# Building the state-space tables of the first stage on one engine, and modulating the tokens on another

## The chip, the cores and the metric

One core of a Trainium2 chip runs the kernel; the other seven are idle. The metric is the device time of one execution in microseconds (us), and the number quoted is the median of three executions.

## What is computed

One layer of a diffusion backbone on 256 latent tokens and 256 context tokens of width 2048, all in float32. The tokens are modulated by a conditioning vector, projected once, mixed by three branches in parallel (long convolution, chunkwise mLSTM, and a bidirectional complex-diagonal state-space model, S5), merged by gates, projected, normalised, and put through a squared-ReLU MLP. Cut to what matters here:

```python
mod_l = split(silu_c @ w_mod[l] + b_mod[l], 6)            # shift, scale, ...
mod_c = split(silu_cc @ w_mod[l] + b_mod[l], 6)
def modulate(h, shift, scale): return h * (1 + scale) + shift
h_ctx, h_lat = modulate(ctx, mod_c[0], mod_c[1]), modulate(x, mod_l[0], mod_l[1])
hy, qk, v, o, gt, u, mg = split(h @ w_in, SPLIT_POINTS)    # for both streams
ab, bb = s5_discretise(a_re, a_im, log_dt, b_re, b_im)     # per direction, group, state
s_t = ab * s_(t-1) + bb u_t;   y_t = Re(c s_t)             # S5, both directions
```

The kernel does the S5 recurrence in chunks of 8 tokens. For that it needs tables built from the weights alone: the complex powers ab^0 to ab^8 of each state, times c (the table Q) and times bb (the table w).

## The kernel before, in words

The work on each engine stands in a fixed order, which a scheduler chose when the kernel was built; each engine takes its instructions strictly in that order. Matrix products of the large projections are done as three products of rounded parts: a weight chunk is loaded by SyncE into a buffer `wr`, ScalarE copies it to its high part `wh`, VectorE subtracts to get the low part `wl`, and TensorE multiplies (`mm`, all at L211). The high part of anything is made at L190 (`act`), the low part at L194 (`split`).

The first stage is the first quarter of a millisecond. It runs three strands side by side:

- **Modulation vectors.** `mod_block` (L395 on) loads `w_mod` in chunks of 512 KB, eight to a block, into ten buffers (four `wr`, three `wh`, three `wl`), multiplies them by the conditioning vectors at L406, copies the result on ScalarE, transposes it with small products, and adds the bias on VectorE (L415, `modc`).
- **Tokens and the K projection.** After each two blocks a group g of four 128-channel slices of both streams can be modulated. `h_group` (L426 on) does this by eight VectorE instructions of 128x256 (L435, `ty<-ty,modc`), then makes four high parts on ScalarE and four low parts on VectorE (tile `t`, two KB wide streams `hc` and `hl`). There are four groups. Three K-projection steps of `w_in` (`part`, L1449 on) follow each group; their partial sums are added on VectorE at L1460.
- **S5 tables.** `s5_params` (L440 on) discretises. `s5_tables` (L540 on) then goes over six channel tiles, two halves of each, and two directions d. `powers` (L525) makes a piece of Q or w by four multiplications with a broadcast operand (L536, L537) and one addition (L538). Direction 0 runs on VectorE, direction 1 on GpSimd. TensorE multiplies Q by a small masked matrix `bb` (L564) and transposes w (L214); ScalarE copies the transposes to `s5wa`; Q goes to memory from GpSimd's queue (L568, tensor QD), the transposes from ScalarE's queue (L583, tensor WA).

The tables are a side strand: `chunk_done` advances them by one step per weight chunk, times a rate (1.0). They are not needed until the S5 branch, hundreds of microseconds later. After the stage, from about 240 us, TensorE runs almost without a pause to the end.

Of the kernel before, what the change touches and what calls it, by code (L numbers as in the profile page):

```python
# [17 lines left out]
P = 128  # L18
# [97 lines left out]
class Kern:  # L116
# [322 lines left out]

    def s5_params(self):  # L440
# [10 lines left out]
        self.work = [self.t(self.br, [P, 1152], f"s5t{d}", 1) for d in range(2)]  # L451
        tmp = self.slices(self.work[0][:, :1104].rearrange("p (a n) -> p a n", n=48))
# [51 lines left out]
        w1, w2 = (self.work[1][:, 384 * i:384 * i + 384].rearrange("p (q c) -> p q c", c=16) for i in range(2))  # L504
# [20 lines left out]
    def powers(self, out, m, d, q, l0, n):  # L525


        e = self.nc.vector if d == 0 else self.nc.gpsimd
        k = q.stop - q.start
        pw = self.pq[:, :, q, :] if d == 0 else self.pq[:, :, q, ::-1]  # L530
        pw = pw[:, :, :, l0:l0 + n]
        t = self.work[d][:, :k * 2 * n * 16].rearrange("p (q s l c) -> p q s l c", q=k, s=2, c=16)
        for s in range(2):
            bcp = lambda i: pw[:, i].unsqueeze(3).to_broadcast([P, k, n, 16])
            bcm = lambda i: m[:, i, q, :].unsqueeze(2).to_broadcast([P, k, n, 16])
            e.tensor_mul(out[:, :, s], bcp(1 + s), bcm(0))  # L536
            e.tensor_mul(t[:, :, s], bcp(s), bcm(1))  # L537
        e.tensor_add(out, out, t)  # L538

    def s5_tables(self):  # L540
# [3 lines left out]
        v = nc.vector  # L544
        for ct in range(CT):
            pk = self.aux([P, 2, P])
            for half in range(2):
                for d in range(2):
                    q = slice(24 * d + 4 * ct + 2 * half, 24 * d + 4 * ct + 2 * half + 2)
                    Q1 = self.t(self.br, [P, 576], f"s5Q{d}", 1)  # L550
                    Q = Q1.rearrange("p (q s n) -> p q s n", q=2, s=2)
                    self.powers(Q.rearrange("p q s (l c) -> p q s l c", c=16), self.s5C, d, q, 0, 9)
                    bb = self.t(self.br, [P, 2, 2, 32], "s5bb", 2)
                    nc.gpsimd.memset(bb, 0.0)
                    for h in range(2):

                        for s in range(2):
                            self.act(bb[64 * h:64 * h + 64, s, :, 16 * h:16 * h + 16],
                                     self.s5B[64 * h:64 * h + 64, s, q, :], scale=1.0 - 2.0 * s)
                    l0 = 0 if d == 0 else 16  # L560
                    for s in range(2):
                        for i in range(2):
                            p = 2 * half + i
                            nc.tensor.matmul(pk[32 * p:32 * p + 32, d, :], bb[:, s, i, :], Q[:, i, s, l0:l0 + P],  # L564
                                             start=d == 0 and s == 0, stop=s == 1, skip_group_check=True,
                                             tile_position=(0, 32 * p))
                    o = 16 - l0
                    nc.gpsimd.dma_start(self.QD[ct, d, :, 2 * half:2 * half + 2], Q[:, :, :, o:o + P])  # L568
                    yield
                wt = []  # L570
                for d in range(2):
                    q = slice(24 * d + 4 * ct + 2 * half, 24 * d + 4 * ct + 2 * half + 2)
                    w = self.t(self.br, [P, 2, 2, P], "s5w", 4)
                    self.powers(w.rearrange("p q s (l c) -> p q s l c", c=16), self.s5B, d, q, d, LC)
                    wt.append(w)
                for i in range(2):
                    wa = self.t(self.br, [P, 4, P], "s5wa", 2)
                    pt = self.aux([P, 4, P])
                    for d in range(2):
                        for s in range(2):  # L580
                            self.tr(pt[:, 2 * d + s, :], wt[d][:, i, s])
                    self.act(wa, pt)
                    nc.scalar.dma_start(self.WA[ct, :, 2 * half + i], wa)  # L583
                yield
            kk = self.t(self.br, [P, 15, 16], "s5kk", 2)
# [6 lines left out]
            yield  # L592
# [65 lines left out]
    def s5_output(self):  # L658
# [8 lines left out]
        for ct in range(CT):  # L667
# [3 lines left out]
            Q = self.t(self.br, [P, 2, 4, 2, P], "s5wq", 2)  # L671
            nc.scalar.dma_start(Q.rearrange("p d q s n -> p d (q s n)"),
                                self.QD[ct].rearrange("d p q s n -> p d (q s n)"))
# [9 lines left out]
            for d in range(2):  # L683
                for s in range(2):
                    for p in range(4):
                        o = 64 * (p % 2)
                        self.nc.tensor.matmul(py[o:o + 64, p // 2, :], xb[:, p, d, s].rearrange("p g j -> p (g j)"),
                                              Q[:, d, p, s, :], start=p < 2 and d == 0 and s == 0, stop=False,
# [885 lines left out]
```

## Time and profile before

| | us |
|---|---|
| median of 3 executions (lowest, highest) | 2039.77 (2035.3, 2040.7) |
| the profiled execution, its own time | 2046.25 |
| its span, from first to last instruction | 2044.3 |
| TensorE busy in the span | 1885.0 |
| VectorE busy | 1342.6 |
| ScalarE busy | 797.7 |
| GpSimd busy | 473.4 |

Busy time is the time in which an engine has an instruction under way, and an instruction that is held up after its start counts as busy. So a long mean for a shape that is short elsewhere is itself a wait. The last column of a group row gives the idle time of the engine just before the group and what ended it. The profiled execution is 6.5 us above the median.

### The profile page before, as it was taken

The numbers are of one execution on the slowest core, as the hardware profiler recorded it, in microseconds if no ns is written. First come the engines' busy times: TensorE is split into PE (matmuls) and PEld (weight loads), VectorE is DVE, ScalarE is ACT, GpSimd is POOL, SyncE is SP. The second block draws the span as 40 slices with busy tenths as digits, with TensorE's granted clock in tenths as the row PEclk, the third lists the DMA queues.
The fourth block names the chain that finished last, engine by engine and source line by source line (L and its number), as shares of the span: only waits on it lengthen the run. The fifth ranks groups of instructions, "written<-read, shape, count | busy, mean of one in ns | idle before, by whom it ended". The sixth has DMA issues, their size and how long they took to land.

```text
span 2044.3 us, 34693 instructions
## 1 busy us (share of the span) xinstructions
PE 1885.0 (92%) x13945; PEld 1716.5 (84%) x13945; DVE 1342.6 (66%) x1842; ACT 797.7 (39%) x1079; POOL 473.4 (23%) x654
## 2 busy tenths in 40 slices
PE   4787899999999896999889998899999999999996
PEld 1555888898998896999769977899989899998986
DVE  8789876655876564455777767866655555555556
ACT  1233333324544332534333443544343334444332
POOL 4777311000015997000343400500000000000001
PEclk8898899999999898999999999999999999999998
DMA  8798667766698675777756876577765566666653
GB/s 311 262 299 285 195 203 221 228 199 184 206 318 272 211 242 172 262 251 243 270 183 217 278 249 218 174 248 229 244 208 190 189 185 181 184 185 230 190 187 115
DMA packets 255200, 455.92 MB, mean 223 GB/s; under 512 B 28789, under 2 KB 75541, under 8 KB 253504
## 3 DMA queue, kind: packets, MB, share of 16 engines
q1 hardware_dynamic: 221824, 382.43, 59.0%
q0 software_dynamic: 12384, 44.54, 6.2%
q10 hardware_dynamic: 20832, 26.75, 3.9%
q8 instruction: 109, 1.79, 0.4%
q14 instruction: 51, 0.42, 0.1%
HBM read 424.75 MB, written 32.05 MB: 223 GB/s over the span
## 4 chain that ended last, share of the span: by engine, by line
PE 64%; DVE 14%; DMA 8%; POOL 8%; issue 4%; ACT 1%; ACTq 0%; POOLq 0%; DVEq 0%; SPq 0%
PE mm L211 57%; DMA wr<-in_w_mod_dram 4%; PE aux L211 4%; DVE wl L194 4%; POOL sc L654 2%; POOL sc L653 2%; POOL t L655 2%; POOL sc L652 2%; DVE t L194 1%; DMA wr<-in_w_in_dram 1%; DVE ty L435 1%; ACT wh L190 1%; DVE mac L1181 1%; DVE s5t L537 1%; DMA s5wq<-WA 1%
## 5 line engine op out<-in xcount | busy, mean ns | idle before, releaser
L211 PE MATMUL mm<-t,wh 128*128 128x256 f32 x5888 | 1102.7, 288 | 24.8 <-ACT wh L190 12.6
L211 PEld LDWEIGHTS mm<-t,wh 128*128 128x128 f32 x5888 | 933.7, 194 | 46.6 <-ACT wh L190 13.9
L194 DVE TENSOR_TENSOR wl<-wr,wh 128x1024 fp32r<-128x1024 f32 (+1 forms) x517 | 657.0, 1277 | 381.6 <-ACT wh L190 380.7
L211 PE MATMUL mm<-t,wl 128*128 128x256 f32 x2944 | 850.1, 289 | 23.3 <-DVE wl L194 23.0
L190 ACT ACTIVATE wh<-wr 128x1024 fp32r<-128x1024 f32 (+1 forms) x517 | 546.4, 1058 | 807.9 <-PE mm L211 577.6
L211 PEld LDWEIGHTS mm<-t,wl 128*128 128x128 f32 x2944 | 571.4, 194 | 37.4 <-DVE wl L194 29.4
L1181 DVE SCALAR_TENSOR_TENSOR mac<-wr,vecs,mac 128x512 f32<-128x512 f32 x240 | 186.8, 778 | 152.7 <-DMA wr<-in_w_mod_dram 150.0
L211 PE MATMUL mm<-wh,t 128*128 128x512 f32 (+1 forms) x960 | 249.3, 349 | 1.7 <-ACT wh L190 1.7
L211 PEld LDWEIGHTS mm<-wh,t 128*128 128x128 f32 x960 | 169.7, 191 | 25.6 <-ACT wh L190 2.7
L211 PE MATMUL mm<-wl,t 128*128 128x512 f32 (+1 forms) x480 | 169.2, 352 | 5.2 <-DVE wl L194 5.2
L211 PE MATMUL mm<-wh,ff 128*128 128x512 f32 (+1 forms) x576 | 155.3, 358 | 0.0
L211 PEld LDWEIGHTS mm<-wh,ff 128*128 128x128 f32 x576 | 101.8, 188 | 17.6
L211 PEld LDWEIGHTS mm<-wl,t 128*128 128x128 f32 x480 | 91.6, 191 | 21.7 <-DVE wl L194 10.5
L211 PE MATMUL mm<-wl,ff 128*128 128x512 f32 (+1 forms) x288 | 103.0, 357 | 0.0
L1403 POOL DMA_DIRECT2D t<-in_ln_g_dram x1 | 0.5, 535 | 358.8 <-PE mm L211 358.8
L211 PE MATMUL mm<-ty,wh 128*128 128x256 f32 x384 | 74.1, 291 | 0.0
L211 PE MATMUL mm<-ty,wl 128*128 128x256 f32 x192 | 57.0, 297 | 6.7 <-DVE wl L194 6.7
L211 PEld LDWEIGHTS mm<-ty,wh 128*128 128x128 f32 x384 | 61.6, 195 | 0.9
L211 PEld LDWEIGHTS mm<-wl,ff 128*128 128x128 f32 x288 | 54.2, 188 | 8.8
L1192 POOL DMA_DIRECT2D mrow<-b x8 | 4.0, 502 | 227.8 <-DVE b L1190 227.8
L211 PE MATMUL aux<-t,t 128*128 128x384 f32 (+3 forms) x160 | 48.8, 422 | 8.0 <-DVE t L1147 3.5
L406 PE MATMUL px<-wr,b 128*32 128x512 f32 x128 | 40.3, 714 | 12.9 <-DVE s5t L335 10.7
(389 smaller groups left out, 1813.6 us busy)
## 6 DMA issues: line engine op xcount, KB each, us to landing
wr<-in_w_ff_dram SPq DMA_DIRECT2D x256, 512.0 KB, 3.9
wr<-in_w_in_dram SPq DMA_DIRECT2D x192, 512.0 KB, 4.7
wr<-in_w_mod_dram SPq DMA_DIRECT2D x160, 512.0 KB, 4.8
wr<-in_w_out_dram SPq DMA_DIRECT2D x32, 512.0 KB, 4.9
wh<-in_w_mod_dram SPq DMA_DIRECT2D x16, 512.0 KB, 6.2
wl<-in_w_mod_dram SPq DMA_DIRECT2D x16, 512.0 KB, 7.8
QD<-s5Q POOLq DMA_DIRECT2D x24, 256.0 KB, 4.9
WA<-s5wa ACTq DMA_DIRECT2D x24, 256.0 KB, 5.2
```

Of the source, the lines that this page charges most:

```text
L190: return self.nc.scalar.activation(out, in_, f, bias=bias, scale=scale)
L194: self.nc.vector.tensor_sub(lo, x, hi.bitcast(F32))
L211: self.nc.tensor.matmul(out, lhsT, rhs, start=start, stop=stop, skip_group_check=True)
L406: nc.tensor.matmul(ps[o:o + 32], self.st[:, k, :], raw[:, kk, :], start=k < 4, stop=k >= KT - 4, skip_group_check=True, tile_position=(0, o))
L435: self.nc.vector.tensor_scalar(h[:, j], h[:, j], self.modc[:, 16 + k, m:m + 1], self.modc[:, k, m:m + 1], op0=ALU.mult, op1=ALU.add)
L537: e.tensor_mul(t[:, :, s], bcp(s), bcm(1))
L652: v.tensor_mul(t1, self.a8[:, 0], S[:, :, :, :, n - 1])
L653: v.tensor_mul(t2, self.a8[:, 1], S[:, :, ::-1, :, n - 1])
L654: v.tensor_add(t1, t1, S[:, :, :, :, n])
L655: v.tensor_add(S[:, :, :, :, n], t1, t2)
L1181: v.scalar_tensor_tensor(acc, x, c, acc, op0=ALU.mult, op1=ALU.add)
L1192: nc.gpsimd.dma_start(self.mrow[which // 3:which // 3 + 1, o:o + 512], brow)
```

## The change

All powers run on VectorE, in pieces of a whole channel tile (four state groups instead of two), for both directions. That makes half as many pieces, each twice as wide: multiplications of 128x576 and 128x512, additions of 128x1152 and 128x1024. GpSimd keeps the memsets of `bb` and the transfers of Q, and gets the transfers of the transposes (WA), which ScalarE's queue issued. The tokens are modulated on ScalarE by an activation with a scale and a bias per partition. The side strand's rate goes from 1.0 to 0.8; it has fewer steps. Buffers: two of 1152 columns for Q (one per direction of 576 before), two of 1024 for w (four of 512), one `s5kk` (two). The layout of QD in memory changes, and its readers with it. In the code of the change the lines of `powers` are L537, L538 and L539, the product is L566, the transfers L570 (QD) and L589 (WA).

```diff
                 for j in range(2):
                     k, m = k0 + j, 1 - s
-                    self.nc.vector.tensor_scalar(h[:, j], h[:, j], self.modc[:, 16 + k, m:m + 1],
-                                                 self.modc[:, k, m:m + 1], op0=ALU.mult, op1=ALU.add)
+                    self.act(h[:, j], h[:, j], AF.Identity, bias=self.modc[:, k, m:m + 1],
+                             scale=self.modc[:, 16 + k, m:m + 1])
                 self.split(hh[:, k0:k0 + 2, :], hlo[:, k0:k0 + 2, :], h)
...
-    def powers(self, out, m, d, q, l0, n):
+    def powers(self, out, m, d, ct, l0, n):
-        e = self.nc.vector if d == 0 else self.nc.gpsimd
-        k = q.stop - q.start
+        v = self.nc.vector
+        q = slice(24 * d + 4 * ct, 24 * d + 4 * ct + 4)
         pw = self.pq[:, :, q, :] if d == 0 else self.pq[:, :, q, ::-1]
         pw = pw[:, :, :, l0:l0 + n]
-        t = self.work[d][:, :k * 2 * n * 16].rearrange("p (q s l c) -> p q s l c", q=k, s=2, c=16)
+        t = self.work[:, :128 * n].rearrange("p (s q l c) -> p s q l c", s=2, q=4, c=16)
+        bcp = lambda i: pw[:, i].unsqueeze(3).to_broadcast([P, 4, n, 16])
+        bcm = lambda i: m[:, i, q, :].unsqueeze(2).to_broadcast([P, 4, n, 16])
         for s in range(2):
-            bcp = lambda i: pw[:, i].unsqueeze(3).to_broadcast([P, k, n, 16])
-            bcm = lambda i: m[:, i, q, :].unsqueeze(2).to_broadcast([P, k, n, 16])
-            e.tensor_mul(out[:, :, s], bcp(1 + s), bcm(0))
-            e.tensor_mul(t[:, :, s], bcp(s), bcm(1))
-        e.tensor_add(out, out, t)
+            v.tensor_mul(out[:, s], bcp(1 + s), bcm(0))
+            v.tensor_mul(t[:, s], bcp(s), bcm(1))
+        v.tensor_add(out, out, t)
...
         for ct in range(CT):
             pk = self.aux([P, 2, P])
-            for half in range(2):
-                for d in range(2):
...
+            wt = []
+            for d in range(2):
+                q = slice(24 * d + 4 * ct, 24 * d + 4 * ct + 4)
+                Q1 = self.t(self.br, [P, 1152], "s5Q", 2)
...
+                self.powers(Q.rearrange("p s q (l c) -> p s q l c", c=16), C, d, ct, 0, 9)
+                bb = self.t(self.br, [P, 2, 4, 32], "s5bb", 2)
...
+                nc.gpsimd.dma_start(self.QD[ct, d], Q[:, :, :, o:o + P])
+                w = self.t(self.br, [P, 2, 4, P], "s5w", 2)
+                self.powers(w.rearrange("p s q (l c) -> p s q l c", c=16), B, d, ct, d, LC)
+                wt.append(w)
+                yield
...
-                    nc.scalar.dma_start(self.WA[ct, :, 2 * half + i], wa)
...
+            for i in range(4):
+                wa = self.t(self.br, [P, 4, P], "s5wa", 2)
+                pt = self.aux([P, 4, P])
+                for d in range(2):
+                    for s in range(2):
+                        self.tr(pt[:, 2 * d + s, :], wt[d][:, s, i])
+                self.act(wa, pt)
+                nc.gpsimd.dma_start(self.WA[ct, :, i], wa)
+                if i % 2:
+                    yield
...
-                self.with_side(side(), 1.0)
+                self.with_side(side(), 0.8)
```

Three places in the order of the instructions. In the rows, `s5t` is the scratch of `powers`, `t_19` and `t_20` are the parts of the two token streams, `ty` the loaded tokens, `aux` and `px` are banks of PSUM, and "x2" stands for two instructions alike.

VectorE, at the second group of tokens. Before:

```order
L536 TENSOR_TENSOR s5Q_111_699<-s5pq_189,s5C_122 128x2x144 x2
L538 TENSOR_TENSOR s5Q_111_699<-s5Q_111_699,s5t_31_129 128x576
L537 TENSOR_TENSOR s5t_31_129<-s5pq_189,s5B_121 128x2x128 x2
L538 TENSOR_TENSOR s5w_793<-s5w_793,s5t_31_129 128x512
L590 TENSOR_TENSOR s5kk_689<-s5kk_689,aux_484 128x16
L537 TENSOR_TENSOR s5t_31_129<-s5pq_189,s5C_122 128x2x144 x2
L536 TENSOR_TENSOR s5w_876<-s5pq_189,s5B_121 128x2x128 x2
L415 TENSOR_TENSOR modc_101<-px_1084,vecs_93 128x8
L435 TENSOR_SCALAR ty_107<-ty_107,modc_101 128x256 x2
L435 TENSOR_SCALAR ty_109<-ty_109,modc_101 128x256 x2
L435 TENSOR_SCALAR ty_108<-ty_108,modc_101 128x256 x2
L435 TENSOR_SCALAR ty_110<-ty_110,modc_101 128x256 x2
```

And of the change:

```order
L539 TENSOR_TENSOR s5w_725<-s5w_725,s5t_133 128x1024
L415 TENSOR_TENSOR modc_101<-px_886,vecs_93 128x8
L538 TENSOR_TENSOR s5t_133<-s5pq_196,s5C_126 128x576 x2
L539 TENSOR_TENSOR s5Q_786<-s5Q_786,s5t_133 128x1152
L538 TENSOR_TENSOR s5t_133<-s5pq_196,s5B_125 128x512 x2
L539 TENSOR_TENSOR s5w_816<-s5w_816,s5t_133 128x1024
L194 TENSOR_TENSOR t_19_102<-ty_107,t_19_102 128x512
```

The eight modulations are gone from here; six instructions of the tables stand between the modulation vector and the first low part.

ScalarE, at the third group of tokens. Before:

```order
L190 ACTIVATE s5wa_1024<-aux_1025 128x512
L583 DMA WA_76<-s5wa_1024 128x512
L190 ACTIVATE b_252_1645<-px_1444 128x512
L190 ACTIVATE s5wa_1032<-aux_1033 128x512
L583 DMA WA_76<-s5wa_1032 128x512
L190 ACTIVATE t_19_102<-ty_107 128x512
L190 ACTIVATE t_20_103<-ty_109 128x512
```

And of the change:

```order
L190 ACTIVATE s5wa_1032<-aux_1033 128x512
L190 ACTIVATE s5wa_1040<-aux_1041 128x512
L190 ACTIVATE b_207_1380<-px_1184 128x512
L190 ACTIVATE ty_107<-ty_107,modc_101 128x256 x2
L190 ACTIVATE ty_109<-ty_109,modc_101 128x256 x2
L190 ACTIVATE ty_108<-ty_108,modc_101 128x256 x2
L190 ACTIVATE ty_110<-ty_110,modc_101 128x256 x2
L190 ACTIVATE t_19_102<-ty_107 128x512
L190 ACTIVATE s5wa_1056<-aux_1057 128x512
L190 ACTIVATE t_20_103<-ty_109 128x512
L190 ACTIVATE s5wa_1064<-aux_1065 128x512
```

All eight modulations stand ahead of the first high part, the WA issues have left, and the third and fourth copy of a tile (`s5wa_1056`, `s5wa_1064`) stand between the high parts; there are two `s5wa` buffers.

GpSimd's queue, at the fourth channel tile of the change; before, the engine's queue in the first tile:

```order
L537 TENSOR_TENSOR s5t_32_130<-s5pq_189,s5C_122 128x2x144 x2
L538 TENSOR_TENSOR s5Q_50_323<-s5Q_50_323,s5t_32_130 128x576
L568 DMA QD_77<-s5Q_50_323 128x4x128
L537 TENSOR_TENSOR s5t_32_130<-s5pq_189,s5B_121 128x2x128 x2
L568 DMA QD_77<-s5Q_60_376 128x4x128
L554 MEMSET s5bb_403 128x128
L538 TENSOR_TENSOR s5w_350<-s5w_350,s5t_32_130 128x512
```

And of the change:

```order
L581 DMA KK_89<-s5kk_826 128x240
L570 DMA QD_77<-s5Q_872 1024x1x128
L589 DMA WA_76<-s5wa_831 128x512
L589 DMA WA_76<-s5wa_839 128x512
L589 DMA WA_76<-s5wa_851 128x512
L556 MEMSET s5bb_1083 128x256
L589 DMA WA_76<-s5wa_859 128x512
L570 DMA QD_77<-s5Q_936 1024x1x128
```

No arithmetic is left on GpSimd; the transfers of Q and of the transposes now share its queue.

## Rows read from the trace of the kernel before

**Rows 1.** The page, busy time of an engine: us, share of the span, instructions.

```profile
PE 1885.0 (92%) x13945; PEld 1716.5 (84%) x13945; DVE 1342.6 (66%) x1842; ACT 797.7 (39%) x1079; POOL 473.4 (23%) x654
```

**Rows 2.** Stretches: length, busy PE, PEld, DVE, ACT, POOL, clock, transfer share, GB/s.

```profile
0.00:43.00 43.00, 20.66 (x90) 5.45 (x90) 35.44 (x138) 5.80 (x18) 14.54 (x33) 0.87 0.95 342
43.00:103.00 60.00, 44.96 (x310) 31.68 (x314) 44.38 (x55) 18.68 (x50) 45.05 (x55) 0.81 0.75 247
103.00:151.00 48.00, 39.18 (x312) 28.31 (x308) 43.00 (x51) 16.27 (x47) 36.37 (x46) 0.93 0.90 295
151.00:208.00 57.00, 41.94 (x320) 30.20 (x312) 53.55 (x59) 20.11 (x52) 44.42 (x60) 0.89 0.87 288
...
240.00:260.00 20.00, 20.00 (x165) 19.28 (x163) 18.09 (x54) 6.40 (x10) 11.95 (x12) 1.00 0.70 224
```

**Rows 3.** Timeline of VectorE, the starts of the four groups: start us, us, what.

```profile
43.04 7.74 DVE L435 TENSOR_SCALAR ty<-ty,modc 128x256 f32<-128x256 f32 x8
...
103.00 3.66 DVE L435 TENSOR_SCALAR ty<-ty,modc 128x256 f32<-128x256 f32 x8
...
151.00 4.82 DVE L435 TENSOR_SCALAR ty<-ty,modc 128x256 f32<-128x256 f32 x6
...
208.11 4.63 DVE L435 TENSOR_SCALAR ty<-ty,modc 128x256 f32<-128x256 f32 x8
```

**Rows 4.** Groups by shape, 0 to 245 us: busy us, mean ns, idle before.

```profile
L194 DVE TENSOR_TENSOR wl<-wr,wh 128x1024 fp32r<-128x1024 f32 x15 | 22.9, 1525 | 0.0
L435 DVE TENSOR_SCALAR ty<-ty,modc 128x256 f32<-128x256 f32 x32 | 21.6, 741 | 0.1
...
L536 DVE TENSOR_TENSOR s5Q<-s5pq,s5C 128x288 f32<-128x288 f32 x24 | 19.2, 838 | 6.1 <-PE aux L564 6.1
L537 DVE TENSOR_TENSOR s5t<-s5pq,s5C 128x288 f32<-128x288 f32 x24 | 18.9, 822 | 0.2
L568 POOL DMA_DIRECT2D QD<-s5Q x24 | 18.8, 784 | 14.2 <-DVE s5Q L538 11.7 <-POOL s5Q L538 2.1 <-POOL s5bb L554 0.3
...
L538 DVE TENSOR_TENSOR s5w<-s5w,s5t 128x512 f32<-128x512 f32 x12 | 17.2, 1430 | 0.3
L536 DVE TENSOR_TENSOR s5w<-s5pq,s5B 128x256 f32<-128x256 f32 x24 | 17.1, 755 | 11.9 <-PE aux L214 11.9
...
L537 DVE TENSOR_TENSOR s5t<-s5pq,s5B 128x256 f32<-128x256 f32 x24 | 16.2, 716 | 0.3
...
L194 DVE TENSOR_TENSOR t<-ty,t 128x512 fp32r<-128x512 f32 x16 | 15.7, 1015 | 0.0
...
L538 DVE TENSOR_TENSOR s5Q<-s5Q,s5t 128x576 f32<-128x576 f32 x12 | 11.7, 972 | 0.2
...
L190 ACT ACTIVATE t<-ty 128x512 fp32r<-128x512 f32 x16 | 10.1, 630 | 15.8 <-DVE ty L435 13.7 <-DMA wr<-in_w_mod_dram 2.1
```

**Rows 5.** Timeline of VectorE, single instructions, most with GpSimd at rest: start, us.

```profile
26.97 0.75 DVE L538 TENSOR_TENSOR s5Q<-s5Q,s5t 128x576 f32<-128x576 f32 x1
...
29.59 0.56 DVE L508 TENSOR_TENSOR s5t<-s5B,s5t 128x384 f32<-128x384 f32 x1
...
35.70 0.69 DVE L538 TENSOR_TENSOR s5w<-s5w,s5t 128x512 f32<-128x512 f32 x1
...
191.01 5.91 DVE L538 TENSOR_TENSOR s5w<-s5w,s5t 128x512 f32<-128x512 f32 x1
...
239.52 1.22 DVE L194 TENSOR_TENSOR wl<-wr,wh 128x1024 fp32r<-128x1024 f32 x1
```

**Rows 6.** ScalarE's groups over the whole span: an activation with scale and bias by partition.

```profile
L190 ACT ACTIVATE b<-b,vecs 128x256 f32<-128x256 f32 x18 | 10.5, 593 | 0.1
```

**Rows 7.** Waits of SyncE's queue, 0 to 240 us: us in total, times, longest.

```profile
SPq L200 <- DVE wl L194: 34.3, 11, 8.9
...
SPq L424 <- DVE t L194: 19.5, 10, 5.1
```

**Rows 8.** Transfers, 0 to 240 us: KB each, median us from issue to landing.

```profile
WA<-s5wa ACTq DMA_DIRECT2D x24, 256.0 KB, 5.2
```

More of the change, by code (lines that the diff above doesn't have):

```diff
@@ L450, in s5_params @@
         are, aim, lg = par[:, 0, :], par[:, 1, :], par[:, 2, :]
-        self.work = [self.t(self.br, [P, 1152], f"s5t{d}", 1) for d in range(2)]
-        tmp = self.slices(self.work[0][:, :1104].rearrange("p (a n) -> p a n", n=48))
+        self.work = self.t(self.br, [P, 1152], "s5t", 1)
+        tmp = self.slices(self.work[:, :1104].rearrange("p (a n) -> p a n", n=48))
         dt_, mag, ph, cs, sn = (tmp(x) for x in ("dt", "mag", "ph", "cs", "sn"))
@@ L503, in s5_params @@
         br, bi = B[:, 0], B[:, 1]
-        w1, w2 = (self.work[1][:, 384 * i:384 * i + 384].rearrange("p (q c) -> p q c", c=16) for i in range(2))
+        w12 = self.t(self.br, [P, 1152], "s5Q", 2)
+        w1, w2 = (w12[:, 384 * i:384 * i + 384].rearrange("p (q c) -> p q c", c=16) for i in range(2))
         for d in range(2):
@@ L544, in s5_tables @@
         v = nc.vector
+        B, C = self.s5B, self.s5C
         for ct in range(CT):
             pk = self.aux([P, 2, P])
-            for half in range(2):
-                for d in range(2):
[L549 to L560, printed above, removed]
-                    for s in range(2):
[L562 to L582, printed above, removed]
-                    nc.scalar.dma_start(self.WA[ct, :, 2 * half + i], wa)
-                yield
@@ L586, in s5_tables @@
+            kk = self.t(self.br, [P, 15, 16], "s5kk", 1)
             kf = pk[:, 0].rearrange("p (l c) -> p l c", c=16)
@@ L591, in s5_tables @@
             nc.gpsimd.dma_start(self.KK[ct], kk.rearrange("p l c -> p (l c)"))
-            yield
+            for i in range(4):
+                wa = self.t(self.br, [P, 4, P], "s5wa", 2)
+                pt = self.aux([P, 4, P])
+                for d in range(2):
+                    for s in range(2):
+                        self.tr(pt[:, 2 * d + s, :], wt[d][:, s, i])
[3 more added lines that the diff above has]
+                    yield
     def s5_spread(self):
@@ L687, in s5_output @@
                         self.nc.tensor.matmul(py[o:o + 64, p // 2, :], xb[:, p, d, s].rearrange("p g j -> p (g j)"),
-                                              Q[:, d, p, s, :], start=p < 2 and d == 0 and s == 0, stop=False,
+                                              Q[:, d, s, p, :], start=p < 2 and d == 0 and s == 0, stop=False,
                                               skip_group_check=True, tile_position=(0, o))
@@ L1414, in run @@
         self.WA = self.t(self.dr, [CT, P, 4, 4, P], "WA")
-        self.QD = self.t(self.dr, [CT, 2, P, 4, 2, P], "QD")
+        self.QD = self.t(self.dr, [CT, 2, P, 2, 4, P], "QD")
         self.mrow = self.t(self.dr, [2, D], "mrow")
```

18 lines of the change are left out of this document (14 added, 4 removed).

## The prediction

> **What bounds the kernel now.** I read the page first: TensorE is busy for 92% of the span [rows 1], so the kernel is a TensorE kernel as a whole, and a change to the tables can only pay where TensorE has holes. The view by stretches shows where. From 240 us on TensorE is busy for 20.00 of 20.00 us at full granted clock; in the three stretches from 43 to 208 us it is busy for 44.96 of 60, 39.18 of 48 and 41.94 of 57 us, at a clock of 0.81 to 0.93 [rows 2]. So the stage ahead of 240 us is the one place to shorten, and what is cut there is cut from the end: afterwards TensorE follows its own fixed order without a pause.
>
> What paces that stage? I cut it where each group of tokens starts to be modulated: 43.04, 103.00, 151.00 and 208.11 us [rows 3]. In those stretches the transfers were busy 0.75, 0.90 and 0.87 of the time, and VectorE 44.38, 43.00 and 53.55 us [rows 2]. Over the first 208 us VectorE is busy for 35.44 + 44.38 + 43.00 + 53.55 = 176.4 us and idle for 31.6. So two resources are nearly full, and the rest of the time goes in short waits between engines.
>
> But VectorE's busy time is not all work. The addition of 128x512 takes 0.69 us when GpSimd is at rest, and 5.91 us once at 191 us [rows 5]; its mean in this stage is 1.43 us, and the one of 128x576 averages 0.97 against 0.75 [rows 4, 5]. The low part of a weight chunk averages 1.525 us here, 1.22 us after the stage [rows 4, 5]. GpSimd is busy for 14.54 + 45.05 + 36.37 + 44.42 = 140.4 of these 208 us, mostly with its half of the powers [rows 2]. The instructions with two operands in on-chip memory are held up while GpSimd computes; that is how I read the surplus.
>
> **The change, part by part.**
>
> *Powers.* VectorE's half costs 19.2 + 18.9 + 17.2 + 17.1 + 16.2 + 11.7 = 100.3 us now [rows 4]. After the change it does both halves alone. From 512 to 1024 columns an unhindered two-operand instruction goes from 0.69 to 1.22 us, 1.035 ns a column [rows 5]; the multiplication of 384 columns with a broadcast operand, 0.56 us, lies on that line [rows 5], so broadcasting costs nothing extra. A piece of Q is then four multiplications of 576 columns at 0.75 and an addition of 1152 at 1.22 + 0.13 = 1.35, a piece of w four of 512 at 0.69 and one of 1024 at 1.22: 3.00 + 1.35 + 2.76 + 1.22 = 8.33 us. Six tiles times two directions: 100.0 us. VectorE does twice the work in the same time: the term is 0, and GpSimd's part is free.
>
> *Low parts.* With GpSimd still, 15 chunks lose 0.305 us each and 16 token low parts 1.015 - 0.69 = 0.325 us each [rows 4, 5]. Eleven of the former and twelve of the latter lie before the fourth group: 3.4 + 3.9 = 7.3 us less on VectorE.
>
> *Modulation.* 32 instructions of 0.741 us leave VectorE [rows 4]; 24 of them lie before the fourth group, 17.8 us. ScalarE gets 32 x 0.593 = 19.0 us [rows 6], and it was busy for only 5.80 + 18.68 + 16.27 + 20.11 = 60.9 of the 208 us [rows 2]. On the path from vector to product it is a trade. The first high part now comes after eight modulations, not two: 6 x 0.593 = 3.6 us later. The last one comes after 8 x 0.593 + 4 x 0.630 = 7.3 us [rows 4, 6], where the modulations alone took 3.66 to 7.74 us before [rows 3] and the low parts followed on a crowded VectorE. I take 0, between +3.6 and -4 us a group.
>
> *VectorE in sum.* It needs 176.4 - 7.3 - 17.8 = 151.3 us up to the fourth group, 25 us less. If it alone paced the stage, 25 us would be the gain; that is one end.
>
> *Transfers.* The same bytes move. Over the three stretches the transfers are busy 0.75 x 60 + 0.90 x 48 + 0.87 x 57 = 137.8 of 165 us [rows 2]. SyncE's queue waited 34.3 us for low parts of chunks and 19.5 us for token low parts [rows 7]; these are what a freer VectorE shortens, and then the transfers are the next bound. At the best share seen among these stretches, 0.90, the 165 us become 153, a gain of 12; at the 0.95 of the first 43 us, 145, a gain of 20. I take the middle, 16. The first 43 us, at a share of 0.95, gain nothing.
>
> *After the fourth group.* Eight modulations take about what they took (4.63 us on VectorE, 8 x 0.593 = 4.7 on ScalarE), four low parts gain 1.3 us: 1 us.
>
> *WA on GpSimd's queue.* Issuing costs 24 x 0.784 = 18.8 us by the like transfers of Q [rows 4], on an engine that loses over 100 us of arithmetic: hidden. What can hurt is the landing, below. Wider pieces, fewer steps at a lower rate and the smaller number of buffers for w I cost at nothing: the tables are wanted only long after the stage, and VectorE waited 11.9 us in all for the transposes to free w, 6.1 us for Q [rows 4]. If that cover goes, those waits at most double, 18 us more.
>
> Sum: 16 + 1 = 17 us. On the profiled execution's 2046.25 us that is 2029; the median stands 6.5 us lower, so 2039.8 - 17 = **2023 us**.
>
> **The rivals.**
>
> 1. *VectorE was the only pace, and the transfers have slack.* For it: in stretch two they ran at 0.75. Against: 0.90 and 0.87 in the next two [rows 2]. Gain 25 + 1 = 26 us: 2014 us.
>
> 2. *The stage is paced by waits that stay.* Each engine's order is fixed, and TensorE takes weight chunks, tokens, Q products and transposes from one line; if the transfers and these waits set the stretches, VectorE's relief only turns into idle time. For it: VectorE was idle 31.6 us of 208 although its queue was long. Against: SyncE waited on VectorE for 53.8 us [rows 7]. No change: 2040 us.
>
> 3. *ScalarE gets stuck behind the transposes: slower.* The third copy of a tile into `s5wa` must wait until the first transfer has landed. That takes 5.2 us today on a queue of its own [rows 8]; on GpSimd's queue it stands behind a transfer of Q of twice the size, 2 x 0.784 us, and its own issue, so 7.6 us. In the new order of ScalarE this copy stands right ahead of a chunk copy, a modulation vector's copy, the high parts of a group or the modulations themselves in five of six tiles. If 6 of the 7.6 us show each time, 30 us are lost against 17 gained: 2053 us. It decides from 17 / 5 = 3.4 us a place. Against: ScalarE is idle for 70% of the stage, and the copies wait mostly for TensorE.
>
> The like transfers of Q were issued in 0.784 us each while VectorE was busy for 85% of the time [rows 2, 4]. The Trainium skill (SBUF — State Buffer, Who interferes with whom) speaks against the new place of WA: a transfer issued on GpSimd needs that engine to write its descriptors, it is locked out while VectorE runs in a two-port mode, and the page advises ScalarE's or SyncE's queue instead; another section gives about 3100 ns where 620 ns would do. By that figure the landing of rival 3 would be some 2.5 us later still, an estimate, and five places with 2.5 us more each would add 12.5 us to the time of rival 3; but the same page says the two-operand instructions of the powers have no such mode, and the rows of Q agree.
>
> **How the numbers follow.** Forecast 0.58; rival 1 0.14; rival 2 0.14; rival 3 0.14. About 0.3%, 6 us, can be told from no change. Forecast and rival 1 are both faster: 0.72; rival 2 is the same: 0.14; rival 3 slower: 0.14. The forecast alone spans 2015 to 2031 (gains of 12 + 1 to 20 + 1, with 4 us of the modulation's trade at either end). To hold 8 in 10 the range reaches down past rival 1 to 2006 (a full group's trade of 4 us twice on top of it) and up over rival 2 with its 6 us to 2047; what lies outside is most of rival 3 and a little below.
>
> **What would show it.** Right: no GpSimd arithmetic before 240 us; multiplications of 576 columns near 0.75 us and additions near 1.35 and 1.22; low parts of chunks at 1.22; the fourth group modulated near 192 us instead of 208; the transfer share of the stretches at 0.90 or more; the later stretches as before. Wrong: powers well above 100 us in sum (then the surplus was not GpSimd's doing); stretches as long as before with VectorE idle more (rival 2); ScalarE waiting on transfers from `s5wa` ahead of a modulation, and WA landing in 8 us or more (rival 3); or a loss after 240 us, which nothing here foresees.

## The result: 31 us faster, and the profile after

| | before | after |
|---|---|---|
| median of 4 executions, us (lowest, highest) | 2039.37 (2035.3, 2040.7) | 2007.92 (2003.74, 2014.18) |
| ratio of the two, 95% interval | | 0.9856 [0.9834, 0.9879] |
| the profiled execution, us | 2046.25 | 2014.18 |
| fourth group of tokens starts at, us | 208.11 | 179.25 |

The medians lie 31.4 us apart; the ratio of the runs puts the gain at 1.44%. Both profiled executions lie 6 to 7 us above these medians. The engines' busy time in the span, from the page of the kernel after:

```profile
PE 1870.4 (93%) x13945; PEld 1707.4 (85%) x13945; DVE 1300.5 (65%) x1810; ACT 803.2 (40%) x1063; POOL 361.7 (18%) x534
```

Against [rows 1], GpSimd lost 112 us of busy time and VectorE 42, although VectorE took over GpSimd's half of the powers. Where the time came from is read from the starts of the groups, on ScalarE now (start us, us):

```profile
44.09 4.04 ACT L190 ACTIVATE ty<-ty,modc 128x256 f32<-128x256 f32 x8 [0.55 <-DVE modc L415]
...
85.69 4.04 ACT L190 ACTIVATE ty<-ty,modc 128x256 f32<-128x256 f32 x8 [3.27 <-DVE modc L415]
...
130.98 4.04 ACT L190 ACTIVATE ty<-ty,modc 128x256 f32<-128x256 f32 x8 [1.35 <-DVE modc L415]
...
179.25 4.04 ACT L190 ACTIVATE ty<-ty,modc 128x256 f32<-128x256 f32 x8 [0.40 <-DVE modc L415]
```

The first group starts a microsecond later than in [rows 3], the fourth 28.9 us earlier: three stretches of 41.6, 45.3 and 48.3 us instead of 60, 48 and 57. The span is 31.9 us shorter, so nine tenths of the gain are made by the fourth group. The same stretches in the view by stretches (columns as in [rows 2]):

```profile
0.00:44.00 44.00, 22.89 (x104) 6.04 (x106) 36.56 (x134) 7.18 (x19) 7.23 (x26) 0.81 0.97 348
44.00:85.70 41.70, 39.35 (x312) 26.52 (x306) 35.59 (x51) 18.82 (x42) 8.80 (x15) 0.96 0.98 337
85.70:131.00 45.30, 36.98 (x312) 28.50 (x316) 40.56 (x55) 18.68 (x46) 10.17 (x18) 0.89 0.97 331
131.00:179.20 48.20, 40.06 (x320) 29.81 (x312) 32.70 (x42) 19.79 (x41) 9.74 (x18) 0.89 0.94 326
...
231.00:251.00 20.00, 20.00 (x165) 18.58 (x164) 12.74 (x48) 9.05 (x11) 0.50 (x1) 1.00 0.33 102
```

Three things are to be seen against [rows 2]. VectorE's busy time in the three stretches fell from 140.9 to 108.9 us. The transfers' share rose from 0.75, 0.90 and 0.87 to 0.98, 0.97 and 0.94. And TensorE, for 944 products instead of 942, was busy for 116.4 us instead of 126.1, at a granted clock of 0.91 instead of 0.87 (means weighted by length, between its two levels of 1.2 and 2.4 GHz), and idle for 18.8 us instead of 38.9. So the stretches became shorter by 20 us of TensorE's waiting and by 10 us in which its products were done sooner.

VectorE's and ScalarE's groups by shape, 0 to 230 us, that answer to [rows 4]:

```profile
L194 DVE TENSOR_TENSOR wl<-wr,wh 128x1024 fp32r<-128x1024 f32 x17 | 20.7, 1218 | 5.1 <-ACT wh L190 5.1
...
L538 DVE TENSOR_TENSOR s5t<-s5pq,s5C 128x576 f32<-128x576 f32 x24 | 17.2, 753 | 0.1
L537 DVE TENSOR_TENSOR s5Q<-s5pq,s5C 128x576 f32<-128x576 f32 x24 | 17.0, 750 | 1.7 <-DMA QD<-s5Q 1.7
...
L539 DVE TENSOR_TENSOR s5Q<-s5Q,s5t 128x1152 f32<-128x1152 f32 x12 | 16.3, 1354 | 0.2
L190 ACT ACTIVATE ty<-ty,modc 128x256 f32<-128x256 f32 x32 | 16.2, 587 | 5.6 <-DVE modc L415 5.6
L538 DVE TENSOR_TENSOR s5t<-s5pq,s5B 128x512 f32<-128x512 f32 x24 | 15.5, 686 | 0.2
L537 DVE TENSOR_TENSOR s5w<-s5pq,s5B 128x512 f32<-128x512 f32 x24 | 15.0, 685 | 7.4 <-PE aux L214 7.4
L539 DVE TENSOR_TENSOR s5w<-s5w,s5t 128x1024 f32<-128x1024 f32 x12 | 14.6, 1219 | 0.1
```

Low parts take 1.218 us instead of 1.525, and an addition of 1024 columns takes 1.219 us where one of 512 took 1.43. What TensorE waited for in the three stretches says it most directly (each row: total us, times, longest; `mm` are the large products, `aux` those of the tables). Before:

```profile
PE aux L564 <- POOL s5Q L538: 9.5, 4, 4.4
PE mm L211 <- DVE wl L194: 7.8, 6, 3.4
PE aux L564 <- DVE s5Q L538: 4.7, 2, 3.4
PE mm L211 <- DVE t L194: 4.3, 3, 2.6
PE mm L211 <- ACT wh L190: 3.4, 2, 2.9
```

After:

```profile
PE mm L211 <- ACT wh L190: 9.6, 3, 6.9
...
PE mm L211 <- DVE t L194: 0.5, 1, 0.5
...
PE mm L211 <- DVE wl L194: 0.3, 1, 0.3
```

The 26.3 us of waiting for VectorE's low parts and for Q, from either engine, have become 0.8. Against that, waits for ScalarE's high parts of chunks (`wh`) grew from 3.4 to 9.6 us; the longest, 6.9 us, stands behind the second group, where e1 below, which modulates on VectorE, has one of 5.3.

### The profile page after: what moved, and what is told of

The parts are those of the page before. It is cut to its first block, busy times and chain, and to the rows that moved or that the text cites. A ratio compares the mean times of both kernels' runs of the same rounds, so it can differ in the third digit from the quotient of the medians.

```text
span 2012.4 us, 34496 instructions
## 1 busy us (share of the span) xinstructions
PE 1870.4 (93%) x13945; PEld 1707.4 (85%) x13945; DVE 1300.5 (65%) x1810; ACT 803.2 (40%) x1063; POOL 361.7 (18%) x534
## 4 chain that ended last, share of the span: by engine, by line
PE 67%; DMA 10%; DVE 9%; POOL 8%; issue 3%; ACT 2%; SPq 0%; ACTq 0%; POOLq 0%; DVEq 0%
PE mm L211 59%; PE aux L211 4%; DMA wr<-in_w_mod_dram 4%; DVE wl L194 3%; DMA wr<-in_w_in_dram 2%; POOL sc L651 2%; POOL sc L653 2%; POOL sc L652 2%; POOL t L654 2%; DMA wr<-in_w_out_dram 1%; ACT wh L190 1%; PE px L406 1%; PE px L211 1%; PE aux L214 1%; DVE mac L1180 1%
## 5 line engine op out<-in xcount | busy, mean ns | idle before, releaser
L194 DVE TENSOR_TENSOR wl<-wr,wh 128x1024 fp32r<-128x1024 f32 (+1 forms) x517 | 649.6, 1263 | 385.9 <-ACT wh L190 385.4
L211 PE MATMUL mm<-wl,t 128*128 128x512 f32 (+1 forms) x480 | 168.0, 350 | 5.5 <-DVE wl L194 5.5
L211 PEld LDWEIGHTS mm<-ty,wl 128*128 128x128 f32 x192 | 36.9, 192 | 9.1 <-DVE wl L194 8.4
```

The costliest lines, as they stand in the source:

```text
L194: self.nc.vector.tensor_sub(lo, x, hi.bitcast(F32))
L211: self.nc.tensor.matmul(out, lhsT, rhs, start=start, stop=stop, skip_group_check=True)
```

## The experiments

The change has two parts, the powers and the modulation. First each alone, then what it is about GpSimd that costs, then what holds the stage now. The fourth group's start, from one profiled execution each, and the time of all kernels follow. The kernel before ran again beside each set of them, with medians between 2035.1 and 2039.4 us, so the ratios are what to compare:

| kernel | fourth group, us | median, us | ratio to before [95% interval] |
|---|---|---|---|
| the change | 179.3 | 2007.9 | 0.9856 [0.9834, 0.9879] |
| e1, powers alone | 177.9 | 2000.5 | 0.9827 [0.9803, 0.9851] |
| e2, modulation alone | 199.2 | 2020.8 | 0.9922 [0.9892, 0.9952] |
| e5, powers on VectorE, narrow pieces | 176.4 | 1997.3 | 0.9810 [0.9787, 0.9833] |
| e6, GpSimd reads | 215.9 | 2048.4 | 1.0063 [1.0042, 1.0084] |
| e7, GpSimd only writes | 181.9 | 2010.2 | 0.9873 [0.9857, 0.9890] |
| e3, WA on ScalarE's queue | 179.8 | 2006.0 | 0.9855 [0.9837, 0.9873] |
| e8, half the powers | 177.2 | 2000.7 | 0.9824 [0.9800, 0.9848] |
| e9, no transfers of WA | 177.8 | 2006.7 | 0.9844 [0.9814, 0.9875] |
| e12, e8 and e9 together | 168.0 | 1992.4 | 0.9792 [0.9766, 0.9818] |
| e11, a quarter of the transposes | 174.5 | 2000.3 | 0.9824 [0.9799, 0.9848] |
| e13, e5 with the tokens on ScalarE | 185.9 | 2008.1 | 0.9863 [0.9839, 0.9887] |
| e14, e5 with the tokens on both | 181.7 | 2001.4 | 0.9824 [0.9801, 0.9846] |

### e1: the powers alone

The changed kernel with the modulation back on VectorE:

```diff
-                    self.act(h[:, j], h[:, j], AF.Identity, bias=self.modc[:, k, m:m + 1],
-                             scale=self.modc[:, 16 + k, m:m + 1])
+                    self.nc.vector.tensor_scalar(h[:, j], h[:, j], self.modc[:, 16 + k, m:m + 1],
+                                                 self.modc[:, k, m:m + 1], op0=ALU.mult, op1=ALU.add)
```

> The change without the move of the modulations: powers on VectorE by whole tiles, tokens modulated on VectorE as before. If the gain of 31 us comes from GpSimd's operand reads no longer holding up VectorE: most of it stays, 2008 to 2018 us, the modulations take about 0.3 us each instead of 0.741 (8 in under 3.5 us), and the stretches between groups stay under 50 us. If it comes from taking the 32 modulations off VectorE: it is gone, 2030 us or more.

The powers alone give 34.6 us on the median of the kernel before beside it, no less than the whole change. The group of the modulation on VectorE, by shape (busy us, mean ns, idle before):

```profile
L435 DVE TENSOR_SCALAR ty<-ty,modc 128x256 f32<-128x256 f32 x32 | 11.0, 419 | 0.1
```

It takes 0.419 us, not the 0.741 of [rows 4] (some 0.3 had been expected): the modulation too had been held up by GpSimd, and once that is gone there is little for ScalarE to relieve. At the fourth group the two kernels can be laid side by side. In the timeline of the change (start us, us, what, idle before and what ended it), ScalarE first, then TensorE:

```profile
179.25 4.04 ACT L190 ACTIVATE ty<-ty,modc 128x256 f32<-128x256 f32 x8 [0.40 <-DVE modc L415]
183.20 1.04 ACT L190 ACTIVATE wh<-wr 128x1024 fp32r<-128x1024 f32 x1
184.14 1.13 ACT L190 ACTIVATE t<-ty 128x512 fp32r<-128x512 f32 x2
```

```profile
176.99 1.05 PE L211 MATMUL px<-consts,b 128*128 128x2 f32 x8 [0.70 <-ACT b L190]
184.81 0.80 PE L211 MATMUL mm<-t,wh 128*128 128x256 f32 x2 [6.76 <-ACT t L190]
186.15 0.58 PE L211 MATMUL mm<-t,wh 128*128 128x256 f32 x1 [0.55 <-DVE t L194]
```

TensorE in e1:

```profile
176.58 1.05 PE L211 MATMUL px<-consts,b 128*128 128x2 f32 x8 [0.15 <-ACT b L190]
...
179.32 0.50 PE L211 MATMUL mm<-t,wh 128*128 128x256 f32 x2 [0.17 <-ACT t L190]
182.34 0.58 PE L211 MATMUL mm<-t,wh 128*128 128x256 f32 x1 [2.51 <-DVE t L194]
```

From the small products of the modulation vector to the run of large ones TensorE needs 9.2 us with the modulation on ScalarE and 5.8 us with it on VectorE, 3.4 us more at this group: on ScalarE eight modulations and a chunk's copy stand ahead of the first high part.

### e2: the modulation alone

The kernel before, with the modulation on ScalarE (the diff of e1, reversed, on L435).

> The kernel before with the modulations alone moved to ScalarE. If GpSimd's reads are the cause: VectorE loses 21.6 us of instructions but its powers stay slow (1.43 us for the addition of 512 columns), and the time falls by 0 to 10 us, 2029 to 2039 us. If the modulation is the cause: 2015 us or less.

It gains 14 us, more than was expected, though less than a cause in the modulation would have given. The powers and low parts stay slow (0 to 235 us):

```profile
L538 DVE TENSOR_TENSOR s5w<-s5w,s5t 128x512 f32<-128x512 f32 x12 | 16.3, 1359 | 0.2
...
L194 DVE TENSOR_TENSOR wl<-wr,wh 128x1024 fp32r<-128x1024 f32 x15 | 22.9, 1528 | 4.4 <-ACT wh L190 4.4
```

So while GpSimd computes, taking 32 held-up instructions off VectorE pays; the parts of the change do not add up, 34.6 and 14.3 against 31.4 together.

### e5: powers on VectorE in the old pieces

One word of the kernel before:

```diff
-        e = self.nc.vector if d == 0 else self.nc.gpsimd
+        e = self.nc.vector
```

> The kernel before with one word changed: both directions of the powers on VectorE, in the old half-tile pieces; modulations on VectorE, WA from ScalarE's queue. If GpSimd's reads are the cause: VectorE does 240 short instructions in about 24 x 4.1 = 98 us, and the time falls by 15 to 30 us, 2010 to 2025 us. If the wider pieces are the cause: VectorE is overloaded with twice the pieces and the time is 2035 us or more.

1997.3 us, better than was expected and better than the change. It needs neither wide pieces nor the new places of the tokens and of WA. Its powers cost VectorE 108.6 us in 240 instructions; the wide ones cost 95.6 us in 120. Those 13 us are not to be seen in the time (e1 differs from the change in the modulation alone and from e5 in the width and what comes with it, and the intervals of e1 and e5 overlap).

### e6 and e7: GpSimd reading, GpSimd writing

e6 is the changed kernel with products and additions on GpSimd behind each piece, into a tile that nobody reads:

```diff
         v.tensor_add(out, out, t)
+        for s in range(2):
...
+            g.tensor_mul(jo, b1, m1)
+            g.tensor_mul(jo, b2, m2)
+            g.tensor_add(jo, jo, jo)
```

> The change, with GpSimd doing about the arithmetic it did before (for each piece four products and two additions of up to 288 columns) into a tile that nobody reads: GpSimd reads on-chip memory again, and nothing waits for its results but its own queue. If reads on GpSimd hold VectorE up: the addition of 1024 columns goes from 1.22 to 2 us or more, the sum of the powers from 96 us to 140 or more, and the time rises by 25 us or more, to 2033 us or more. If GpSimd mattered only as a link that others waited for: VectorE's means stay within 10% of the change's and the time stays below 2018 us.

Groups by shape, 0 to 240 us:

```profile
L550 POOL TENSOR_TENSOR junk<-s5pq,s5B 128x256 f32<-128x256 f32 x24 | 28.1, 1170 | 9.6 <-issue 8.3
L538 DVE TENSOR_TENSOR s5Q<-s5pq,s5C 128x576 f32<-128x576 f32 x24 | 26.4, 1138 | 0.0
...
L194 DVE TENSOR_TENSOR wl<-wr,wh 128x1024 fp32r<-128x1024 f32 x13 | 19.9, 1534 | 4.8 <-ACT wh L190 4.7
```

The whole gain is gone and more. The multiplication of 576 columns goes from 0.75 to 1.14 us, the addition of 1024 columns from 1.22 to 1.59, the powers from 95.6 to 136.3 us in sum, the low part back to 1.53: a little less than was expected for the powers, more in the time. VectorE does all powers here, and GpSimd's dummies take 146 us where its half of the powers took 113 in the kernel before, so that the time ends above the one before. e7 puts 13 memsets there instead:

```diff
         v.tensor_add(out, out, t)
+        for _ in range(13):
+            self.nc.gpsimd.memset(self.junk, 0.0)
```

> The changed kernel, with 13 memsets of 288 columns on GpSimd behind each piece of the powers: GpSimd is kept busy and its queue is held up, but it reads nothing from on-chip memory. If it is GpSimd's reads of operands that hold VectorE up, the powers stay near 96 us in sum and the low parts of chunks near 1.22 us, the groups of tokens start within 2 us of those of the changed kernel, and the time is within 6 us of its 2008. If any work on GpSimd does it, or if it was the delay of the transfers on GpSimd's queue that cost time with the reading dummies, it goes most of the way to the 2048 us of those: over 2025, with powers over 120 us in sum in the first case and near 96 us in the second.

```profile
L542 POOL MEMSET junk<- 128x288 f32 x312 | 107.9, 346 | 14.8
...
L194 DVE TENSOR_TENSOR wl<-wr,wh 128x1024 fp32r<-128x1024 f32 x16 | 19.5, 1219 | 2.6 <-ACT wh L190 2.6
...
L538 DVE TENSOR_TENSOR s5Q<-s5pq,s5C 128x576 f32<-128x576 f32 x24 | 17.1, 752 | 0.0
```

GpSimd is busy with them for 108 us, its transfers stand behind them, and nothing on VectorE moves: 0.752 and 1.219 us, and a time that cannot be told from the change's. So it is GpSimd's reading of operands, not its being busy and not its delayed queue. The Trainium skill (SBUF — State Buffer, Who interferes with whom) states just this pair: a VectorE instruction with two operands in on-chip memory contends with a GpSimd instruction that reads there, and not with one that only writes. The traces of e6 and e7 agree: 1.14 us beside arithmetic that reads, 0.75 beside memsets.

### e3: WA back on ScalarE's queue

```diff
-                nc.gpsimd.dma_start(self.WA[ct, :, i], wa)
+                nc.scalar.dma_start(self.WA[ct, :, i], wa)
```

> The changed kernel, with the transfers of the transposes (WA) issued on ScalarE's queue again. ScalarE waited 15.8 us in six waits for WA transfers in the changed kernel, and the landing took 6.2 us. Theory (the stage is held by the transfers' busy time, ScalarE has room): within 4 us of the changed kernel, 2004 to 2012, whatever the landing becomes. Rival (the queue matters): the landing falls to 5.2 us or less, ScalarE's waits for it fall below 5 us, and 5 us or more are gained, 2003 or less. Second rival: each issue costs ScalarE 0.6 us, 14 us over the stage, which shows as a loss of over 4 us.

No difference in time, although ScalarE's waits for these transfers fell from 15.8 to 6.3 us. The landing of a WA transfer took 6.2 us on GpSimd's queue in the change and 6.1 us on ScalarE's here. An issue took ScalarE some 0.48 us, less than the second rival had it, and showed in no time either.

### e8, e9 and e12: less VectorE, fewer bytes, and both

e8 leaves out, in the changed kernel, the second products and the additions of the powers:

```diff
             v.tensor_mul(out[:, s], bcp(1 + s), bcm(0))
-            v.tensor_mul(t[:, s], bcp(s), bcm(1))
-        v.tensor_add(out, out, t)
```

> The changed kernel without the second products and without the additions of the powers (that part of the tables is left out): VectorE loses 24 x 0.75 + 24 x 0.69 + 12 x 1.35 + 12 x 1.22, some 64 us, of the stage. If the stage is now held by the transfers (share 0.96 in the three stretches), the groups start at most 5 us earlier at the fourth and the time is 2002 to 2008. If VectorE still paces it, its 110 busy us of 135 in the three stretches fall by some 45, and the fourth group starts 15 us or more earlier: 1993 or less.

e9 leaves out the transfers of the transposes; the S5 branch reads Q in their place (that line is not shown):

```diff
-                nc.gpsimd.dma_start(self.WA[ct, :, i], wa)
```

> The changed kernel without the transfers of the transposes to memory (WA is not written; the S5 branch reads Q in its place, with as many bytes): 6.3 MB less of some 45 MB between the first and the fourth group, at 340 GB/s 18.5 us of the transfers' time, of which 3/4 lie before the fourth group. If the stage is now held by the transfers, the fourth group starts 8 to 14 us earlier and the time falls to 1994 to 2002. If VectorE or the waits between engines hold it, the share of the transfers falls below 0.90 with the stretches unchanged, and the time stays within 4 us of 2008.

Between 44 and 178 us VectorE is busy for 51.8 us in e8, against 107.7 in the change. Yet the fourth group comes only 2 us earlier: the rival by which VectorE alone still paces the stage falls. But e9 speaks just as well against the transfers. The three stretches of e9:

```profile
43.70:85.00 41.30, 39.77 (x326) 26.89 (x322) 34.38 (x49) 19.90 (x44) 5.54 (x10) 0.94 0.93 315
85.00:131.40 46.40, 39.91 (x323) 29.52 (x318) 41.55 (x56) 19.55 (x49) 5.99 (x11) 0.89 0.85 292
131.40:177.80 46.40, 37.46 (x300) 28.22 (x294) 32.71 (x43) 18.92 (x37) 4.93 (x11) 0.93 0.84 278
```

The share fell to 0.93, 0.85 and 0.84 and the stretches stayed as they were. Neither theory of mine held alone, so e12 leaves out both in one kernel.

> The changed kernel without the second products and additions of the powers and, in the same kernel, without the transfers of the transposes to memory (the S5 branch reads Q in their place): both kinds of relief at once, each of which alone left the fourth group at 177 to 178 us. If VectorE and the transfers take turns as the bound (each covers for the other), the fourth group now starts 8 us or more earlier, before 170 us, and the time falls to 1993 or less. If neither bounds the stage any more, it stays at 175 to 179 us and the time is that of the kernel with half the powers, 1997 to 2004.

```profile
44.50:91.30 46.80, 40.24 (x340) 30.12 (x338) 20.75 (x34) 23.96 (x58) 8.61 (x14) 0.89 0.92 317
91.30:130.10 38.80, 35.06 (x310) 26.86 (x313) 16.64 (x27) 15.49 (x37) 3.43 (x6) 0.96 0.90 321
130.10:168.00 37.90, 32.56 (x237) 23.95 (x231) 12.49 (x15) 15.14 (x25) 1.49 (x6) 0.95 0.88 295
```

Now the fourth group starts 11.3 us before that of the change, where the parts gave 2.0 and 1.4. TensorE has 1040 products behind it there in all four kernels. (The three stretches, 123.5 us instead of 135.2, flatter e12 a little: 55 more of these products stand ahead of its first group.) For the 1040 products TensorE is busy for 134.1 us instead of 139.3, at a granted clock of 0.93 instead of 0.89, and idle for 33.9 instead of 40.0. Against the change's median 15.5 us are gained where the parts gave 7 and 1; by the ratios it is 13 against 6.5 and 2.4, and with intervals of some 5 us either way the time does not tell both together from the sum of the parts. The start of the fourth group does, as far as one execution each goes: in e3 and e7, whose times cannot be told from the change's, it lies within 2.6 us of the change's. So I read it that after the change VectorE and the transfers cover for each other: relieve one, and the other holds the stage.

### e11: fewer transposes on TensorE

Only one of four transposes of a piece is made, and ScalarE copies it four times:

```diff
-                        self.tr(pt[:, 2 * d + s, :], wt[d][:, s, i])
-                self.act(wa, pt)
+                        if d == s == 0:
+                            self.tr(pt[:, 0, :], wt[d][:, s, i])
+                self.act(wa, pt[:, :1, :].to_broadcast([P, 4, P]))
```

> The changed kernel with one of four transposes of each s5wa piece made on TensorE and copied four times by ScalarE (three quarters of the transposes are left out, so part of the tables is not right): TensorE loses 72 transposes, at 8 in 1.0 to 1.24 us some 10 us, of which 7 to 8 us lie before the fourth group. Theory (after the change it is TensorE with its fixed order that sets the length of the stage, since neither 14 us less of transfers nor 37 us less of VectorE moved the fourth group by more than 2 us): the fourth group starts at 170 to 174 us instead of 179 and the time falls by 6 us or more against 2008. Rival (the length is set by waits between engines that no one engine's load changes): it starts within 2 us of 177 to 179, and the time stays above 2003.

The fourth group starts at 174.5 us and the three stretches take 130.9 us, 4.3 less than in the change, where TensorE has 7.4 us less to do up to the fourth group: between theory and rival in the stage. The median falls by 7.6 us, as the theory had it, but its interval overlaps that of the change. TensorE's own load counts in the stage, for about half of what was taken out.

### e13 and e14: where to modulate, with GpSimd quiet

e13 is e5 with the modulation on ScalarE (as in e2). e14 splits it:

```diff
+                    if s:
+                        self.act(h[:, j], h[:, j], AF.Identity, bias=self.modc[:, k, m:m + 1],
+                                 scale=self.modc[:, 16 + k, m:m + 1])
+                    else:
...
```

> The kernel before with all powers on VectorE in the old narrow pieces (1997.3 by itself) and with the tokens modulated on ScalarE too: the second part of the change, on top of the first. Theory (with GpSimd's reads gone VectorE modulates in 0.42 us a piece and needs no relief, while on ScalarE eight modulations stand ahead of the first high part): 3 to 10 us slower than 1997, 2000 to 2007, as 2008 against 2000 with the wide pieces. Rival (relief of VectorE still counts): 1997 or less.

> The kernel before with all powers on VectorE in the old narrow pieces, and of each group's eight modulations four on VectorE (one stream) and four on ScalarE (the other), side by side: the first high part can start after 4 x 0.42 = 1.7 us instead of 3.3 (VectorE alone) or 4.0 (ScalarE alone). If the lead from the modulation vector to the first product is what separates the variants, 0 to 6 us faster than the 1997.3 of VectorE alone: 1991 to 1997. If it is the load of ScalarE that costs, between the two: 1997 to 2004.

e13 is 10.8 us slower than e5, and the two intervals do not meet: with GpSimd quiet the modulation on ScalarE is a loss, in the narrow pieces surely, in the wide ones (2007.9 against 2000.5, intervals that overlap a little) probably. In e13 TensorE again waits at the fourth group:

```profile
184.57 1.05 PE L211 MATMUL px<-consts,b 128*128 128x2 f32 x8 [0.70 <-ACT b L190]
191.42 0.80 PE L211 MATMUL mm<-t,wh 128*128 128x256 f32 x2 [5.80 <-ACT t L190]
```

The split lies between, with an interval that overlaps those of both. The idea that the lead to the first high part is all that counts finds no support: its four and four take less time than eight on either engine, and it does not beat e5.

## Why the prediction was right, and which term was too small

The forecast was 17 us, the result 31.4. The sign, the place and the cause, GpSimd holding VectorE up, were as argued; the size was not. The time lies 2 us above the lower end of the range, and that it lies inside is in part luck: the range reached down to 2006 by allowing 8 us of gain from the modulation's trade, which cost time instead, while the transfers gave more than they were allowed.

- **Where the time is.** Right. The fourth group starts 28.9 us earlier, and nothing is lost behind it: TensorE is busy for 20.00 of 20.00 us at full clock from 231 us on. It does not run without a pause to the end, though, as I had it: between 600 and 1500 us it is idle for 74.0 us before and 75.7 after. What the stage gained reached the end because these pauses hardly changed.
- **Powers.** Right. By the means of the rows above (0.753 and 0.750, 1.354, 0.686 and 0.685, 1.219) a piece of each table costs 8.32 us, forecast 8.33. But the forecast set twelve such sums, durations added up, against 100.3 us of busy time; in busy time the powers take 95.6 us, so the term was a gain of 5 us and not 0. That GpSimd was the cause is shown by e6 and e7.
- **Low parts.** Right: 1.218 us.
- **Transfers.** This step failed: "At the best share seen among these stretches, 0.90, the 165 us become 153, a gain of 12; at the 0.95 of the first 43 us, 145, a gain of 20. I take the middle, 16." The measured term is 29.9 over the three stretches. The shares became 0.98, 0.97 and 0.94, above both ends; and the busy time of the transfers for nearly the same bytes (44.8 MB, 45.4 before), which I held at 137.8 us, fell to 0.98 x 41.7 + 0.97 x 45.3 + 0.94 x 48.2 = 130.1 us. At the new share 137.8 us of transfers would have filled 143 us, a gain of 22; the other 8 us are the shorter busy time, whose cause no run isolates. A share seen in a stretch where something else holds up the transfers is no ceiling for the stretch where it doesn't. SyncE's queue waited for VectorE (0 to 240 us, as [rows 7]):

```profile
SPq L424 <- DVE t L194: 16.7, 7, 5.3
SPq L200 <- DVE wl L194: 14.9, 7, 5.8
```

31.6 us of such waits are left of 53.8.
- **VectorE in sum.** Too small as well: up to the fourth group it is busy for 145.4 us, 31 less than before, not 25 less. Idle it is for 33.8 us, about what it was (31.6). So the stage became shorter by nearly what VectorE lost, and the 26 us of rival 1 are the nearest number. Its mechanism does not follow from that: the transfers have no slack in these stretches, and in e8, where VectorE is busy for 85.3 us up to the fourth group, 60 less than in the change, the group starts 2 us earlier.
- **The next bound.** Half right. The transfers are full after the change, but they are not the sole bound: without a part of them (e9) the group starts 1.4 us earlier. That they share it with VectorE is the reading of e12, and e11 shows TensorE's own load beside them.
- **Modulation.** Taken as 0 on the path. It costs 11 us in e13 against e5, and in the change probably some 6 us, by its ratio against that of e1. The 3.4 us at the fourth group are close to the +3.6 that the forecast had as its upper bound a group. What I missed is that the 0.741 us of [rows 4] is itself a held-up duration: counting 17.8 us of relief on VectorE, I counted a relief of which 24 x 0.32 = 7.7 us came from GpSimd's silence anyway.
- **GpSimd's part is free.** More than free. I counted it on VectorE alone. TensorE had waited 9.5 us for GpSimd's own Q, which I did not look up.
- **Rival 2 (waits that stay).** Wrong: waits on VectorE and GpSimd went from TensorE's list.
- **Rival 3 (ScalarE stuck behind WA).** Its place is there, its price is not. The landing took 6.2 us, not 7.6 (columns: KB each, median us from issue to landing):

```profile
WA<-s5wa POOLq DMA_DIRECT2D x24, 256.0 KB, 6.2
```

ScalarE waited for it six times, 15.8 us in all; in e3, without GpSimd's queue, it waited 6.3 us and the time was the same. The warning of the Trainium skill (SBUF — State Buffer, Who interferes with whom) against transfers issued on GpSimd, which it ties to VectorE's two-port modes, was not borne out by any row here: 6.2 us on the one queue and 6.1 on the other.

Still open: e5 reaches the fourth group 2.9 us before the change, with 1012 products behind it instead of 1040, and its profiled span (1995.8 us) is 16.6 us shorter. Between 178 and 208 us its TensorE is busy for 27.0 us against 22.7, which is the modulation's place; some 9 us come later, where both do the same work: between 600 and 1500 us TensorE is idle for 66.0 us in e5 and for 75.7 in the change. Executions of one kernel differ by as much as 10 us (the change: 2003.74 to 2014.18), and no run here tells such a spread from an effect of the order.

## What to carry to other kernels

Work that is moved to an idle engine is not free when both engines read the same memory: compare the duration of one shape in a stretch where the other engine rests with its mean where it works, for every shape on the path and not only for those of the change. Put twice the work on the engine that was held up, and it can come out even, while whoever waited for the other engine is served sooner. And when a relief is done, price the next one again: the modulation on ScalarE gained 14 us while GpSimd computed and, with narrow pieces, lost 11 us once it was quiet. The fastest complete kernel here by its median is the one-word change of e5; its interval overlaps those of e1 and e14.

## What the runs showed of the hardware

- A VectorE instruction with one operand and two scalars per partition (128x256) took 0.741 us beside GpSimd's arithmetic and 0.417 to 0.419 without it, so it is not only the two-operand forms that are held up. No run here shows what memsets on GpSimd do to it.
- GpSimd's reads held up two-operand instructions of VectorE, its writes did not: 312 memsets, 107.9 us, left the multiplication at 0.752 us; arithmetic of 146 us brought it to 1.05 to 1.14.
- The transfers' rate at full share (rate over share, which is rounded) was 325 to 337 GB/s in the three stretches of the kernels with GpSimd arithmetic (before, e2, e6) and 329 to 357 in those of the others, mostly above 337. The two overlap, and no run isolates why.
- In the three stretches about as many products kept TensorE busy for 126.1 us at a mean granted clock of 0.87 before (942, with 38.9 us of pauses) and for 116.4 us at 0.91 in the change (944, with 18.8 us of pauses). The change's timeline shows it in small: after the pause of 6.76 us at the fourth group the pairs of products start 0.64 us apart at first, and 0.36 us apart from about 191 us on. The granted clock is 0.50 (1.2 GHz) between 186.2 and 190.5 us and 1.00 (2.4 GHz) between 190.9 and 195.0.

```profile
188.66 0.63 PE L211 MATMUL mm<-t,wh 128*128 128x256 f32 x2
...
189.31 0.63 PE L211 MATMUL mm<-t,wh 128*128 128x256 f32 x2
...
191.43 0.40 PE L211 MATMUL mm<-t,wh 128*128 128x256 f32 x2
...
191.79 0.40 PE L211 MATMUL mm<-t,wh 128*128 128x256 f32 x2
```
